# A RetNet and short-convolution decoder on one core: the norms' scales spread by transposes of whole tiles instead of products with the identity

## The chip, the core and the metric

The kernel runs on one core of a Trainium2 chip. The core has five engines with a queue each: TensorE (PE, with its weight loads as PEld), VectorE (DVE), ScalarE (ACT), GpSimd (POOL) and SyncE (SP). The engines run their own queues in order and wait for each other by semaphores. DMA transfers are issued from SP, ACT and POOL and run beside them. The metric is the device time of one execution in microseconds, the median of several runs; less is better. The granted TensorE clock is 0.999 on this core, so nothing here is throttled.

## The reference, cut to what matters

The program is one inference step of a two-layer decoder with d_model 1024 on 512 prompt tokens and 8 sequences of 4 new tokens each, together 544 token columns. Layer 0 mixes by a gated short convolution, layer 1 by retention; a SwiGLU block of width 2816 follows each; a last norm ends it.

```
def rmsnorm(x, g):
    y = xf * lax.rsqrt(jnp.mean(xf * xf, axis=-1, keepdims=True) + RMS_EPS)
    return y * g
for i in range(DEPTH):
    h = rmsnorm(x, norm_mix[i])
    m, st = short_conv_mixer(h, ...) if i % 2 == 0 else retention_mixer(h, ...)
    x = x + m
    x = x + swiglu(rmsnorm(x, norm_ffn[i]), ffn_w_gate[i], ffn_w_up[i], ffn_w_down[i])
return rmsnorm(x, final_norm), ...
```

There are five norms. Each needs, for every token, one number: the reciprocal root of the mean square over the 1024 features.

## The kernel before, in words

**Layout.** Activations lie transposed: eight tiles `x[0]` to `x[7]` of 128 features (partitions) by 544 tokens (columns). A PSUM bank holds 512 float32 columns, so the tokens are cut in two halves of `HT` = 272. A norm's scale differs by token, so by column, and must stand in every one of the 128 partitions before VectorE can multiply with it. That spread copy is the tile `R` (128 x 2 x 272).

**How a scale is made** (`rms_scale`, line 256, a generator whose steps are woven between the products of a stage). The squares are summed over the eight tiles in `sqacc`. Then five products (line 272) with `sqacc` as the stationary operand turn 128 tokens at a time from columns into a column: `ms[:, tt]` holds the means of 128 tokens, one per partition. VectorE adds epsilon (line 245), GpSimd raises to the power -1/2 (line 248), and the result is the small tile `rN` with one column per 128 tokens. To get from that column to a spread row, `spread` (line 250) takes the column `rN[:, tt]`, broadcast over 128 columns, as the stationary operand, and the identity matrix `ident` as the moving one. Six such products (lines 279 to 283) fill the two halves of 272 columns: whole tiles of 128, cut ones of 16, 112 and 32, since 272 is no multiple of 128. ScalarE copies both halves to `R` (line 284).

This happens four times: for layer 0's mixer (profiled at 34 us), layer 0's SwiGLU (206 us), layer 1's mixer (561 us, in `ahead`) and layer 1's SwiGLU (1055 us). The final norm has its own code (`scale`, line 915): each half of the tokens gets three products (lines 933 and 934), and VectorE multiplies the output straight out of PSUM (line 949); the stores follow on SP's and ACT's queues.

**The matrix products.** All large products are split: a float32 operand is written as a high part and a low part of a faster type, and three products replace one. Two weight matrices and two activation tiles at a time are multiplied by seven instead of eight block products (`Job`, line 364; products on line 386). A job's weights are prepared by `weights7` (line 320): two loads on SP's queue into tiles `w` (line 333), four sums on VectorE (lines 336 to 339), high parts on ScalarE (lines 315 and 202), and low parts in two ways. One half of a low part is a subtraction on VectorE (line 316). The other half is a negated copy on ScalarE (line 317), to which an accumulating DMA on POOL's queue adds the weight itself (line 318). A job's products come in the order 1 (first half of the first pair), then 6, 5 and 2 in an order given by the stage (2 is the second half of the first pair), 7, and at the end 3 and 4. ScalarE and VectorE add up the blocks from PSUM (lines 445 and 447). `run` (line 422) prepares the next job while the present one is multiplied.

**The order.** The program is written in one sequence, but the order on each engine is made by a scheduler that plans with its own estimates of durations, and fixed when the program is built. Pins (`issue_after`) hold a few places. A change of a few instructions can so move others far from it.

**The convolution stage**, the first, holds three plain products per feature pair, then eight jobs of the kind above. In its jobs, `take` (line 615) copies a job's last block from PSUM on ScalarE (line 618); for some jobs the convolution taps follow (lines 561 to 573), and `mixed_in` (line 576) splits the result (lines 209 to 211, with an accumulating DMA of its own).

Of the kernel before, what the change touches and what calls it, by code (L numbers as in the profile page):

```python
# [12 lines left out]
P = 128  # L13
D = 1024
KT = D // P
SEQ = 512
NB = 8
DS = 4
NS = NB * DS
# [4 lines left out]
HT = T // 2  # L24
# [28 lines left out]
def hybrid_decode_kernel(ctx: ExitStack, tc: tile.TileContext, a: dict, o: dict):  # L53
    nc = tc.nc
# [6 lines left out]
    def nm(s):  # L61
        uid[0] += 1
        return f"{s}_{uid[0]}"
# [3 lines left out]
    kinds, at = ["m"], [0]  # L67
# [5 lines left out]
    def psum():  # L73

        kind = kinds[0][at[0] % len(kinds[0])]
        at[0] += 1
        if kind == "s":
            return [bank(), bank()]
        return ps.tile([P, 2, 512], F32, tag="mm", name=nm("mm"), bufs=2)

    def bank():
        return ps.tile([P, 512], F32, tag="sm", name=nm("sm"), bufs=4)

    def half(pt, hf):
        return pt[hf] if isinstance(pt, list) else pt[:, hf, :]

    def each(fn, pt, *aps):

        if isinstance(pt, list):
            for hf in range(2):  # L90
                fn(pt[hf][:, :HT], *[ap[:, hf, :] for ap in aps])
        else:
            fn(pt[:, :, :HT], *aps)
# [6 lines left out]
    mask_s, ident, mean_w = rest[:, :NS], rest[:, NS : NS + P], rest[:, NS + P :]  # L100
# [21 lines left out]
    def g_fin(kt):  # L122
        return vec[:, 72 + kt : 73 + kt]
# [10 lines left out]
    rN = resid.tile([P, 6], F32, tag="rN", name="rN")  # L134
# [107 lines left out]
    def rsqrt(out, var, n, eps=None):  # L242

        if eps is None:
            nc.vector.tensor_scalar_add(out, var, EPS)
        else:
            nc.vector.tensor_add(out, var, eps)
        nc.gpsimd.tensor_tensor(out, out, expo[: out.shape[0], :n], op=ALU.pow)

    def spread(out, tt, lo, hi):  # L250

        return nc.tensor.matmul(
            out, rN[:, tt : tt + 1].to_broadcast([P, P]), ident[:, lo:hi], start=True, stop=True, skip_group_check=True
        )

    def rms_scale(sample=False, pt=None, rest=4):

        n = 6 if sample else 5  # L260
        pt = pt or psum()
        ms = half(pt, 0)[:, 496:502]
        cols = [slice(tt * P, (tt + 1) * P) for tt in range(4)] + [slice(T - P, T), slice(SEQ, T)]
        for tt in range(n):
            lhs = sqacc[:, cols[tt]]
            if tt == 5:
                lhs = sqlast[:, :P]
                nc.vector.tensor_copy(
                    lhs.rearrange("p (g c) -> p g c", c=NS),
                    sqacc[:, SEQ:].unsqueeze(1).to_broadcast([P, P // NS, NS]),  # L270
                )
            nc.tensor.matmul(ms[:, tt : tt + 1], lhs, mean_w[:, 0:1], start=True, stop=True)
            if tt < n - 1:
                yield
        rsqrt(rN[:, :n], ms[:, :n], n)
        for _ in range(rest):
            yield

        for tt, hf, at, lo, hi in (
            (0, 0, 0, 0, P), (1, 0, P, 0, P), (2, 0, 2 * P, 0, HT - 2 * P),  # L280
            (2, 1, 0, HT - 2 * P, P), (3, 1, 3 * P - HT, 0, P), (4, 1, SEQ - HT, P - NS, P),
        ):
            spread(half(pt, hf)[:, at : at + hi - lo], tt, lo, hi)
        each(lambda p, r: nc.scalar.activation(r, p, AF.Copy), pt, R)

    def drain(steps):
        for _ in steps:
            pass
# [165 lines left out]
    with ExitStack() as c0:  # L454
# [134 lines left out]
        c, b = temp("c"), temp("b")  # L589
        nc.gpsimd.memset(u[:, :, NSLOT : NSLOT + 2], 0.0)  # L590
        steps = rms_scale(rest=5)
        pts = [start()]
        for d, pt in zip((b, c), pts[0]):
# [68 lines left out]
        for i, n in enumerate(PAIRED[0]):  # L662
            if i < 2:
                wh, wl, pt = early[i]
                project(pt, wh, wl, 0, yh, yl, first=False, ks=(KT - 2, KT - 1))
            else:
                wh, wl = load_piece(a["cvout"][n], KT * P)
                pt = psum()
# [4 lines left out]
    def ffn(layer, next_gain, then=None):  # L673
        with ExitStack() as c1:
# [198 lines left out]
            def after(i):  # L873
                if i in behind:
                    later[behind[i]]()

            steps = rms_scale(rest=9)
            run(jobs, (5, 6, 2), after, steps)
            drain(steps)
# [8 lines left out]
    def final(ms, acts, group_weights, fp, tp):  # L888

        ah, al = acts  # L890
        ws = [group_weights(n, ms) for n in range(KT - LATE, KT)]

        sums = {}

        def products(hf):
            c = slice(hf * HT, (hf + 1) * HT)
            for n in range(KT - LATE, KT):
                wh, wl = ws[n - KT + LATE]
                pt = [None, None]
                pt[hf] = bank()  # L900
                project(pt, wh, wl, 0, ah, al, hfs=(hf,))
                nc.vector.tensor_add(x[n][:, c], x[n][:, c], half(pt, hf)[:, :HT])
                square_sum(n, tp, "gu", 4, c=c, add=nc.vector, join=not hf)
                yield

        def gained(hf):

            c = slice(hf * HT, (hf + 1) * HT)
            y = [fp.tile([P, 4, HT], F32, tag="f", name=nm("ya")), tp.tile([P, 4, HT], F32, tag="gu", name=nm("yb"))]
            for kt in range(KT):  # L910
                with tc.issue_after(last_square[0].ins) if hf and kt == KT - 2 else ExitStack():
                    nc.scalar.activation(y[kt // 4][:, kt % 4, :], x[kt][:, c], AF.Copy, scale=g_fin(kt))
            return y

        def scale(hf):
            pt = bank()
            mq = pt[:, 496:499]

            of = (sqacc, sqlast)[: hf + 1]
            for t in of:  # L920
                for i, at in enumerate((0, P, HT - P)):
                    cols = slice(hf * HT + at, hf * HT + at + P)
                    last_sum[hf] = nc.tensor.matmul(
                        mq[:, i : i + 1], t[:, cols], mean_w[:, 0:1], start=t is of[0] and (hf == 0 or i == 0),
                        stop=t is of[-1], skip_group_check=True,
                    )
                if t is not of[-1]:
                    yield
            with tc.issue_after(first_product[0].ins) if hf else ExitStack():
                nc.vector.tensor_scalar_add(rN[:, :3], mq, EPS)  # L930
            powers[hf] = nc.gpsimd.tensor_tensor(rN[:, :3], rN[:, :3], expo[:, :3], op=ALU.pow)
            yield
            for i, (lo, hi) in enumerate(((0, P), (0, P), (3 * P - HT, P))):
                last_spread[0] = spread(pt[:, i * P : i * P + hi - lo], i, lo, hi)
            sums[hf] = pt[:, :HT]

        def copied(hf):

            with tc.issue_after(last_square[0].ins):
                nc.scalar.activation(R[:, hf, :], sums[hf], AF.Copy)  # L940

        def out(hf, y, w):

            yy = y[w // 2][:, w % 2 * 2 : w % 2 * 2 + 2, :]
            if w == 0:
                for i in range(2):
                    nc.gpsimd.tensor_tensor(yy[:, i, :], yy[:, i, :], R[:, hf, :], op=ALU.mult)
            else:
                made = nc.vector.tensor_mul(yy, yy, sums[hf].unsqueeze(1).to_broadcast([P, 2, HT]))
                first_product[0] = first_product[0] or made  # L950
            q = nc.sync if w % 2 or hf == 0 else nc.scalar
            last_store[0] = q.dma_start(o["yT"][hf][:, 2 * w : 2 * w + 2], yy)

        last_sum, last_spread, powers, first_product, last_store = {}, [None], {}, [None], [None]

        def idle(n, ins):

            with tc.issue_after(ins):
                wm = bank()
                for _ in range(n):  # L960
                    last_spread[0] = nc.tensor.matmul(wm[:, :P], ones, ones, start=True, stop=True)

        drain(products(0))
        first, second = scale(0), products(1)
        next(second)
        next(first)
        y0 = gained(0)
        drain(second)
        drain(first)
        out(0, y0, 1)  # L970
        with tc.issue_after(first_product[0].ins):
            copied(0)
        rest = scale(1)
        with tc.issue_after(last_spread[0].ins):
            next(rest)
        next(rest)
        idle(5, last_sum[1].ins)
        y1 = gained(1)
        out(0, y0, 2)
        out(0, y0, 3)  # L980

        with tc.issue_after(last_store[0].ins), tc.issue_after(powers[1].ins):
            out(0, y0, 0)
        drain(rest)
        copied(1)
        for w in range(4):
            out(1, y1, w)
# [763 lines left out]
```

## Time and profile before

| | |
|---|---|
| runs | 1411.15, 1411.09, 1410.4 us |
| median | 1411.09 us |
| profiled execution, span from first to last instruction | 1409.1 us |
| PE busy | 1396.3 us (99%), 10,476 matmul records |
| DVE, ACT, POOL busy | 1132.7, 821.7 and 213.9 us |
| DMA | 233.82 MB, mean 166 GB/s |

The profiled execution is known by its span; the median of the timed runs lies 2.0 us above it, which is what stands around the first and the last instruction. The profile shows for each instruction its engine, its line, what it writes and reads, its start and its duration; in the timeline, the first column is the start and the second the duration of the (merged) row, and brackets give the idle time of the engine before it and what ended it. Matmuls overlap, so a row's duration is longer than the distance to the next row's start; that distance is what it costs.

### The profile page before, as it was taken

The page shows a single profiled execution, that of the slowest core. Times are in us where ns is not written, and L with a number is a line of the kernel's source. Part 1 is how long each engine was busy: PE and PEld are TensorE (multiplying, and loading weights), DVE is VectorE, ACT ScalarE, POOL GpSimd, SP SyncE. Part 2 cuts the span into 40 slices and gives each one's busy share as a digit, 9 for nine tenths or more (in the row PEclk, how much of TensorE's full clock was granted, in tenths as well). Part 3 has the DMA queues.
Part 4 walks back from the last instruction along what each step waited for, and adds up shares of the span by engine and source line. Part 5 has one row for each costly group of instructions (what it writes and reads, how often), then busy time and mean ns, then how long its engine had stood idle before and what let it go on. Part 6 is the DMA issues. An engine that isn't in the chain of part 4 may idle for free.

```text
span 1409.1 us, 26606 instructions
## 1 busy us (share of the span) xinstructions
PE 1396.3 (99%) x10476; PEld 1319.9 (94%) x10476; DVE 1132.7 (80%) x1929; ACT 821.7 (58%) x1281; POOL 213.9 (15%) x248
## 2 busy tenths in 40 slices
PE   9999999999999999999999999999999999999997
PEld 9999999999999999999877877887899999999997
DVE  6987879898989878767867586585798898989884
ACT  7666567677677557677532313213387767667654
POOL 0111011222221204111000000000111222121212
PEclk9999999999999999999999999999999999999999
DMA  6476347768686745677666365465676777777742
GB/s 206 121 166 166 107 110 158 173 163 185 143 196 149 171 108 158 176 199 203 197 216 232 120 212 179 139 240 179 201 152 151 168 170 172 154 184 157 163 108 87
DMA packets 99246, 233.82 MB, mean 166 GB/s; under 512 B 9744, under 2 KB 33312, under 8 KB 98736
## 3 DMA queue, kind: packets, MB, share of 16 engines
q1 hardware_dynamic: 67984, 167.60, 38.3%
q0 software_dynamic: 28688, 56.61, 23.5%
q10 hardware_dynamic: 2448, 7.91, 1.5%
q8 instruction: 82, 1.34, 0.4%
q14 instruction: 44, 0.36, 0.1%
HBM read 191.97 MB, written 28.42 MB: 156 GB/s over the span
## 4 chain that ended last, share of the span: by engine, by line
PE 93%; DVE 4%; DMA 1%; ACT 1%; issue 1%; POOL 0%; SPq 0%; DVEq 0%; POOLq 0%; ACTq 0%
PE sm L386 43%; PE mm L386 16%; PE mm L187 14%; PE sm L187 4%; PE sm L1251 2%; PE sm L1252 2%; PE sm L1253 2%; PE sm L175 2%; PE sm L177 2%; PE sm L176 1%; PE sm L1463 1%; DVE S L1486 1%; PE mm L1259 1%; PE mm L1412 0%; DVE ol L203 0%
## 5 line engine op out<-in xcount | busy, mean ns | idle before, releaser
L386 PE MATMUL sm<-oh,wh 128*128 128x272 f32 x856 | 247.8, 290 | 0.5 <-DVE b L447 0.5
L386 PE MATMUL sm<-ol,wh 128*128 128x272 f32 x856 | 246.2, 288 | 0.0
L386 PE MATMUL sm<-oh,wl 128*128 128x272 f32 x856 | 246.1, 287 | 0.0
L202 ACT ACTIVATE h<-w 128x1024 fp32r<-128x1024 f32 (+3 forms) x170 | 136.6, 804 | 105.8 <-PE mm L386 92.7
L203 DVE TENSOR_TENSOR l<-w,h 128x1024 fp32r<-128x1024 f32 (+3 forms) x170 | 153.5, 904 | 28.0 <-ACT h L202 25.0
L315 ACT ACTIVATE wh<-w 128x1024 fp32r<-128x1024 f32 (+1 forms) x134 | 133.7, 998 | 56.0 <-PE sm L386 48.3
L386 PEld LDWEIGHTS sm<-oh,wh 128*128 128x128 f32 x856 | 161.3, 188 | 2.0 <-DVE b L447 0.9
L386 PEld LDWEIGHTS sm<-oh,wl 128*128 128x128 f32 x856 | 161.1, 188 | 0.0
L386 PEld LDWEIGHTS sm<-ol,wh 128*128 128x128 f32 x856 | 160.9, 188 | 0.1
L386 PE MATMUL sm<-parts,wh 128*128 128x272 f32 x736 | 142.5, 288 | 0.0
L202 ACT ACTIVATE wh<-w 128x1024 fp32r<-128x1024 f32 (+3 forms) x76 | 67.6, 897 | 117.2 <-PE mm L187 62.0
L318 POOL DMA_DIRECT2D wl<-in_ffgu_dram x87 | 81.9, 941 | 327.9 <-ACT wl L317 135.5
L386 PE MATMUL mm<-oh,h 128*128 128x272 f32 x396 | 115.5, 292 | 0.0
L386 PEld LDWEIGHTS sm<-parts,wh 128*128 128x128 f32 x736 | 115.5, 188 | 0.0
L386 PE MATMUL mm<-oh,l 128*128 128x272 f32 x396 | 113.4, 286 | 0.0
L386 PE MATMUL mm<-ol,h 128*128 128x272 f32 x396 | 113.2, 286 | 0.0
L316 DVE TENSOR_TENSOR wl<-w,wh 128x512 fp32r<-128x512 f32 (+1 forms) x134 | 87.1, 650 | 26.5 <-ACT wh L315 26.2
L386 PE MATMUL sm<-parts,wl 128*128 128x272 f32 x368 | 106.1, 288 | 0.2 <-DMA wl<-in_rtqk_dram 0.2
L317 ACT ACTIVATE wl<-wh 128x512 fp32r<-128x512 f32 (+1 forms) x173 | 102.9, 595 | 2.0
L203 DVE TENSOR_TENSOR wl<-w,wh 128x1024 fp32r<-128x1024 f32 (+3 forms) x76 | 79.5, 1055 | 13.4 <-ACT wh L202 13.0
L187 PE MATMUL mm<-parts,wh 128*128 128x272 f32 x488 | 82.6, 291 | 0.9 <-ACT wh L202 0.9
L386 PE MATMUL sm<-oh,h 128*128 128x272 f32 x284 | 82.3, 290 | 0.3 <-ACT oh L202 0.2
(382 smaller groups left out, 3841.2 us busy)
## 6 DMA issues: line engine op xcount, KB each, us to landing
w<-in_ffgu_dram SPq DMA_DIRECT2D x66, 512.0 KB
wl<-in_ffgu_dram POOLq DMA_DIRECT2D x87, 256.0 KB, 5.2
S<-in_rets_dram SPq DMA_DIRECT2D x16, 1024.0 KB
out_rets_dram<-S SPq DMA_DIRECT2D x16, 1024.0 KB
w<-in_ffdn_dram SPq DMA_DIRECT2D x36, 384.0 KB
cb<-in_ffgu_dram SPq DMA_DIRECT2D x22, 512.0 KB
w<-in_cvin_dram SPq DMA_DIRECT2D x21, 512.0 KB
wl<-in_ffdn_dram POOLq DMA_DIRECT2D x48, 192.0 KB, 4.7
```

The lines of the kernel that those rows point to most:

```text
L175: nc.tensor.matmul(out, lh, rh, start=start, stop=False, skip_group_check=True)
L177: last_product[0] = nc.tensor.matmul(out, ll, rh, start=False, stop=stop, skip_group_check=True)
L187: last_product[0] = nc.tensor.matmul(half(pt, hf)[:, :HT], w[:, c], act[k][:, hf * HT : (hf + 1) * HT], start=(first and k == ks[0] and i ...
L202: h = nc.scalar.activation(dh, src, AF.Copy)
L203: last_low[0] = nc.vector.tensor_sub(dl, src, dh.bitcast(F32))
L315: nc.scalar.activation(wh, w, AF.Copy)
L316: last_mixed[0] = nc.vector.tensor_sub(wl[:, :n], w[:, :n], wh[:, :n].bitcast(F32))
L317: nc.scalar.activation(wl[:, n:], wh[:, n:].bitcast(F32), AF.Copy, scale=-1.0)
L318: nc.gpsimd.dma_start(wl[:, n:], src[:, 1, :] if len(src.shape) == 3 else src[:, n:], accum_op=ALU.add)
L386: last = nc.tensor.matmul(out, w[:, c], b, start=(first and j == 0 and i == 0), stop=(j == len(self.ks) - 1 and i == 2), skip_group_check= ...
L1251: nc.tensor.matmul(out, xh[kt][:, ts_], wh[:, cw], start=(kt == 0), stop=False)
L1252: nc.tensor.matmul(out, xh[kt][:, ts_], wl[:, cw], start=False, stop=False)
```

## The change

`spread` becomes a transpose of the whole broadcast tile (`tensor.transpose`, a matmul in transpose mode) where the wanted columns begin at the tile's first column, and stays a product with part of the identity where they do not. The list of cuts changes with it: whole tiles of 128 are written even where fewer columns are wanted. In the first half, tile 2 writes columns 256 to 383, of which 256 to 271 are read. In the second half, tile 2's last 112 columns stay a product, and the last tile, which holds the last 128 tokens, is written whole over columns that tile 3 has written just before with the same values. In the final norm the third spread of a half is written whole and overlaps the second.

```
-    def spread(out, tt, lo, hi):
-        return nc.tensor.matmul(
-            out, rN[:, tt : tt + 1].to_broadcast([P, P]), ident[:, lo:hi], start=True, stop=True, skip_group_check=True
-        )
+    def spread(out, tt, lo=0):
+        column = rN[:, tt : tt + 1].to_broadcast([P, P])
+        if lo == 0:
+            return nc.tensor.transpose(out, column, ident)
+        return nc.tensor.matmul(out, column, ident[:, lo:], start=True, stop=True, skip_group_check=True)
...
-        for tt, hf, at, lo, hi in (
-            (0, 0, 0, 0, P), (1, 0, P, 0, P), (2, 0, 2 * P, 0, HT - 2 * P),
-            (2, 1, 0, HT - 2 * P, P), (3, 1, 3 * P - HT, 0, P), (4, 1, SEQ - HT, P - NS, P),
+        for tt, hf, at, lo in (
+            (0, 0, 0, 0), (1, 0, P, 0), (2, 0, 2 * P, 0), (2, 1, 0, HT - 2 * P), (3, 1, 3 * P - HT, 0), (4, 1, HT - P, 0),
         ):
-            spread(half(pt, hf)[:, at : at + hi - lo], tt, lo, hi)
+            spread(half(pt, hf)[:, at : at + P - lo], tt, lo)
...
-            for i, (lo, hi) in enumerate(((0, P), (0, P), (3 * P - HT, P))):
-                last_spread[0] = spread(pt[:, i * P : i * P + hi - lo], i, lo, hi)
+            for i, at in enumerate((0, P, HT - P)):
+                last_spread[0] = spread(pt[:, at : at + P], i)
```

In all, 26 of the 30 products become transposes, and four products of 112 columns stay. The built order of the instructions changes in two ways: the edited instructions themselves, and, in the convolution stage behind the first group, the order in which PE, DVE, ACT and POOL take the work of the first jobs. SP's order and all other stages keep theirs.

## The prediction

> **What bounds the kernel now.** I read the page from its head: span, busy shares, clock, chain.
>
> ```profile
> span 1409.1 us, 26606 instructions
> PE 1396.3 (99%) x10476; PEld 1319.9 (94%) x10476; DVE 1132.7 (80%) x1929; ACT 821.7 (58%) x1281; POOL 213.9 (15%) x248
> PEclk9999999999999999999999999999999999999999
> PE 93%; DVE 4%; DMA 1%; ACT 1%; issue 1%; POOL 0%; SPq 0%; DVEq 0%; POOLq 0%; ACTq 0%
> ```
>
> TensorE is the bound nearly everywhere: 99% busy, 93% of the chain that ended last, clock granted in full. So time taken out of PE's queue shortens the kernel, and an operand that comes late lengthens it at once. Two things have to be priced: the edited instructions on PE, and the order of everything else. The built order of the changed kernel differs from that of before far from the edit, in the convolution stage.
>
> **Part 1: the four groups of six products in the norms.** The view of the spread's line counts its instructions, and the timeline shows the first group.
>
> ```profile
> L252 PE MATMUL mm<-cb,rN x36: 182/275/377, 33.9 to 1056.0; 128*128 128x128 f32 x18, 128*128 128x16 f32 x6, 128*128 128x112 f32 x6, 128*128 128x32 f32 x6
> L252 PE MATMUL sm<-cb,rN x24: 182/275/376, 561.2 to 1400.5; 128*128 128x128 f32 x14, 128*128 128x16 f32 x6, 128*128 128x112 f32 x2, 128*128 128x32 f32 x2
> ...
> 33.12 0.66 PE L187 MATMUL mm<-parts,wh 128*128 128x272 f32 x4
> 33.62 0.41 PE L187 MATMUL mm<-parts,wl 128*128 128x272 f32 x2
> 33.86 1.42 PE L252 MATMUL mm<-cb,rN 128*128 128x128 f32 x12
> 35.12 0.76 PE L187 MATMUL mm<-parts,wh 128*128 128x272 f32 x4
> 35.72 0.41 PE L187 MATMUL mm<-parts,wl 128*128 128x272 f32 x2
> ...
> 205.58 1.53 PE L252 MATMUL mm<-cb,rN 128*128 128x128 f32 x12
> 561.19 1.42 PE L252 MATMUL sm<-cb,rN 128*128 128x128 f32 x12
> 1054.83 1.42 PE L252 MATMUL mm<-cb,rN 128*128 128x128 f32 x12
> ```
>
> There are 36 + 24 = 60 matmul records for 30 products: each float32 product runs as two passes. The twelve passes hold PE from 33.86 to 35.12, 1.26 us, and the four products behind take 0.60 (35.12 to 35.72) where they usually take 0.50 (33.12 to 33.62). So a group costs 1.36 us; the other three last as long or a little longer.
>
> What a transpose costs is seen at the keys' transposes, the same instruction with the same identity:
>
> ```profile
> 705.62 1.04 PE L1306 MATMUL mm<-cb,rot 128*128 128x128 f32 x8
> 706.41 0.48 PE L1252 MATMUL sm<-wl,parts 128*128 128x512 f32 x1
> 706.73 0.40 PE L1253 MATMUL sm<-wh,parts 128*128 128x512 f32 x1
> 706.97 0.39 PE L1251 MATMUL sm<-wh,parts 128*128 128x512 f32 x1
> ```
>
> Eight records for eight transposes: one pass each. From 705.62 to 706.73 is 1.11 us, less 0.24 for the one product in between (706.73 to 706.97): 0.87, or 0.11 per transpose, entry and exit included. After the change a group is five transposes (0.55) and one 112-column product, still two passes (12 passes in 1.26 us: 0.21). That is 0.76 instead of 1.36: 0.60 less. Bounds: 0.42 (transposes at 0.14) to 0.70 (at 0.09). The whole-tile transposes write 112 columns more than the cut products (to no reader) and overwrite 96 twice, on one engine in order, so no wait is added. Three of the groups stand in stretches whose order is unchanged: -0.6 each, -1.8 us. The scales reach their readers earlier, which is worth nothing there: PE does not wait for them.
>
> **Part 2: the two groups of three at the end.**
>
> ```profile
> 1396.58 0.74 PE L252 MATMUL sm<-cb,rN 128*128 128x128 f32 x6
> 1396.78 0.44 DVE L902 TENSOR_TENSOR x<-x,sm 128x272 f32<-128x272 f32 x1
> 1397.25 0.43 ACT L234 ACTIVATE sqlast<-x 128x272 f32<-128x272 f32 x1 [0.18 <-DVE x L902]
> 1397.84 0.81 PE L923 MATMUL sm<-cb,sqlast 128*128 128x1 f32 x6
> 1399.90 0.84 PE L252 MATMUL sm<-cb,rN 128*128 128x128 f32 x6
> 1400.78 0.40 ACT L940 ACTIVATE R<-sm 128x272 f32<-128x272 f32 x1 [1.86 <-PE sm L252]
> DMA  0000000000079207999389998999996000000000
> ```
>
> The first group becomes 0.3 shorter (six passes, half of 1.26, are 0.63; three transposes, 0.33), but the last sums behind it need the squares that ACT ends at 1397.68, so only some 0.1 is gained. The second stands bare between POOL's power and the copy: 0.84 becomes 0.33 + 0.22 = 0.55, gain 0.3. Behind it the stores keep the DMA engines full (last row: 1395 to 1409.2 in 40 slices, nearly all nines from 1400.3 on), so at best the 0.4 arrives and at worst none. I take -0.25.
>
> **Part 3: the order of the convolution stage.** The first group also gives -0.6 at 34 us. But the scheduler has ordered the stage behind it anew, for some 360 products of its seven-product jobs (line 386). Job 2, the third, is where it matters. The built orders, abbreviated:
>
> ```
> ACT before: L315 wh_910 | L317 wl_911 | L202 h4_788 | L315 wh_920 | L618 h_760<-sm_747
> ACT after:  L202 h4_788 | ... L315 wh_910 | L618 h_760<-sm_747 | L317 wl_911
> PE: wl_911's second half first read by product 207 of L386 before, by product 149 after
>     job 0's last (sm_747): products 99-110 before, 104-115 after
> ```
>
> The first half of wl_911 comes from DVE and is early in both. The second half is made by ACT at L317 and then by POOL's accumulating DMA (L318). In the new order L317 stands behind L618, which waits for job 0's last product, and the reader is pulled 58 products ahead. The rows, of before:
>
> ```profile
> 57.81 0.41 PE L386 MATMUL sm<-parts,wh 128*128 128x272 f32 x2
> 72.34 0.29 PE L386 MATMUL sm<-ol,h 128*128 128x272 f32 x1
> 76.44 0.41 PE L386 MATMUL sm<-parts,wh 128*128 128x272 f32 x2
> 83.20 0.28 PE L386 MATMUL mm<-ol,h 128*128 128x272 f32 x1
> 90.08 0.29 PE L386 MATMUL sm<-oh,wl 128*128 128x272 f32 x1
> ...
> 68.72 0.63 ACT L317 ACTIVATE wl<-wh 128x512 fp32r<-128x512 f32 x1
> 71.91 1.06 ACT L315 ACTIVATE wh<-w 128x1024 fp32r<-128x1024 f32 x1 [0.88 <-PE sm L386]
> 72.87 0.38 ACT L618 ACTIVATE h<-sm 128x272 f32<-128x272 f32 x1
> 73.15 0.62 ACT L317 ACTIVATE wl<-wh 128x512 fp32r<-128x512 f32 x1
> ...
> 69.64 0.86 POOL L318 DMA_DIRECT2D wl<-in_cvin_dram  x1 [1.61 <-PE sm L386]
> ...
> DMA to landing us min/median/max: 3.7/6.5/7.7
> ...
> wl<-in_cvin_dram POOLq DMA_DIRECT2D x1, 256.0 KB, 5.4
> ```
>
> These PE rows are products 1, 115, 148-149, 200 and 255 of the stage; PE never starves here before, so place gives time. All shift by -0.6. Product 115 ends at 72.34 + 0.29 - 0.6 = 72.03. Then L618 (0.28 to the next start), L317 (0.62) and 0.29 from L317's end (69.35) to POOL's issue (69.64): issue at 73.2 instead of 69.64. Product 149 is due at 76.56 - 0.6 = 75.96. Landing takes 3.7 at the least, so PE waits at least 0.95 us; at 7.7 it waits 4.95. I take 5.4, the one issued at 54.3 (last row) with one weight load beside it, as here: landing at 78.6, **a wait of 2.65 us**. Queued behind it on PE is everything.
>
> The next job has the same pattern: its L317 now waits for product 200 (83.20 + 0.28 - 0.6 = 82.9), through L315 (0.97), L618, L317 and the issue to 85.1; the reader is product 255, due at 89.5, 4.4 later. At 3.7 it is in time, at 7.7 it costs 3.3. The engines' queue is emptier there, since a weight load has moved; I take nothing.
>
> PE being late covers later waits in turn:
>
> ```profile
> 109.82 0.52 PE L386 MATMUL mm<-parts,h 128*128 128x272 f32 x2 [0.32 <-ACT b L445]
> 114.45 0.39 PE L386 MATMUL sm<-oh,wh 128*128 128x272 f32 x1 [0.48 <-DVE b L447]
> ```
>
> If ACT and DVE are not late with PE, 0.8 us goes here; if they are, nothing. They wait for PE's sums themselves, so I take 0.4. SP's order is unchanged; on POOL one store-like accumulate (L211) moves behind a weight's, which nobody awaits within 10 us.
>
> **The sum**, against the profiled 1409.1: -0.6 + 2.65 - 0.4 in the first stage, -1.8 in three groups, -0.25 at the end: -0.4 us. The median of the runs, 1411.09, lies 2.0 above this span; I predict **1410.7 us**.
>
> **The rivals.**
> *The new wait is hidden* (20%). For it: the smallest landing, 3.7, and the two old waits. Then -0.6 - 1.8 - 0.25 = -2.65, 1408.4; with 0.8 of old waits gone, 1407.6. Against: even 3.7 leaves 0.95 in my walk.
> *The accumulating DMAs are slow* (20%, slower). With 6.5 us, the median of this stretch, in both places the waits are 3.75 and 2.1: -2.65 + 5.85 = +3.2, 1414.3. It decides from a sum of waits of 5.5 us on. Against: the queue is less crowded at 73 us than before.
> *Transposes do not pipeline* (2%). The row of L1306 gives 0.27 as one transpose's own duration; taken one after another a group costs 5 x 0.27 + 0.21 = 1.56, 0.2 more than now, and the sum of my terms becomes -0.4 + 4 x 0.8 = +2.8, 1413.9. The eight in 1.04 us speak against it, and the clock row has no dip where L1306 runs. The Trainium skill, page "TensorE: Matmul & The Clock Gate", section "Part 4: PE-mode transpose", gives about 275 ns for a transpose in one kernel and says the clock gate does not count transposes as busy, which would speak against this change; this case's trace agrees with the duration as a latency, not as a rate.
> That the change does nothing (transposes as two passes) I hold excluded: L1306 shows one record each.
>
> **How the numbers follow.** 58% the forecast (1408.6 with a landing of 3.7 and both old waits gone, to 1413.4 with 7.7 and none gone), 20% hidden, 20% slow, 2% unpipelined. What a measurement of this kernel can tell from no change is about 0.2%, 2.8 us: 1408.3 to 1413.9. The hidden case (1407.6 to 1408.4) lies for two thirds beyond its lower end, 0.13, and the forecast's lower end is nearer to it than the runs' scatter of 0.75 us, 0.03: faster 0.16. The slow case lies mostly beyond the upper end, with the unpipelined one half: 0.18, and 0.03 of the forecast's upper end in the same way: slower 0.21. The range, 1407.8 to 1414.4, reaches into both.
>
> **What would show it.** Five single records and two passes per group, PE 0.76 us in it; L618 ahead of the third job's L317; an idle time of PE near 76 us ended by DMA wl, 1 to 5 us long. Wrong it is if that wait is missing, if a second one stands near 90 us, or if waits at 110 and 114 us grow instead of shrinking.

## The result, and the profile after

The changed kernel takes 1414.74 us in the median of nine runs (1413.08 to 1415.95), the kernel before 1410.45 beside it (1409.88 to 1411.31): a ratio of 1.0028 with an interval of 1.0018 to 1.0037. It is slower by 4 us; 1410.7 was forecast, with 1414.4 as the upper end. The profiled execution of the changed kernel, at 1413.33 us one of its quicker ones, has this page; the groups' last columns are the idle time before them and what ended it.

```profile
span 1411.6 us, 26557 instructions
...
PE 1395.2 (99%) x10450; PEld 1317.2 (93%) x10450; DVE 1133.0 (80%) x1929; ACT 820.4 (58%) x1281; POOL 213.4 (15%) x248
...
PE 85%; DVE 4%; DMA 2%; ACT 1%; issue 1%; POOL 0%; DVEq 0%; SPq 0%; POOLq 0%; ACTq 0%
...
L386 PE MATMUL sm<-parts,wl 128*128 128x272 f32 x368 | 106.7, 290 | 3.2 <-DMA wl<-in_cvin_dram 3.0
```

PE's busy time has become 1.1 us less (1396.3 before), the span 2.5 us more: what was saved is there, and more has been lost in waiting. The chain holds DMA for 2% instead of 1%. (PE's share of it, 85% against 93%, is 91% in the second trace of the same kernel, so nothing is read from it.) The list of PE's waits (total, times, longest) names them:

```profile
PE sm L386 <- DMA wl<-in_cvin_dram: 3.0, 1, 3.0
PE sm L485 <- DVE expo L108: 1.1, 1, 1.1
PE sm L386 <- DVE c L447: 0.8, 1, 0.8
PE mm L187 <- ACT wh L202: 0.5, 1, 0.5
```

The first and the third are new; the waits of before for `b` (L445 and L447) are gone. The timeline shows the first one as the prediction walked it: L618 ahead of L317, the DMA issued at 73.82, PE at the reader from 75.7 on, and its work resumed at 78.91, 5.1 us after the issue. What holds L618 is L315 ahead of it on ACT, which waited for PE until 71.67.

```profile
71.67 1.06 ACT L315 ACTIVATE wh<-w 128x1024 fp32r<-128x1024 f32 x1 [4.17 <-PE sm L386]
72.63 0.38 ACT L618 ACTIVATE h<-sm 128x272 f32<-128x272 f32 x1
72.91 0.62 ACT L317 ACTIVATE wl<-wh 128x512 fp32r<-128x512 f32 x1
73.82 0.86 POOL L318 DMA_DIRECT2D wl<-in_cvin_dram  x1 [6.26 <-ACT wl L317]
75.47 0.41 PE L386 MATMUL sm<-parts,wh 128*128 128x272 f32 x2
78.91 0.39 PE L386 MATMUL sm<-parts,wl 128*128 128x272 f32 x1 [3.02 <-DMA wl<-in_cvin_dram]
```

The third, near 96 us, was not forecast. VectorE's addition to `c`, for which PE waits, stands in the new order behind two sums of the next weights, and the first of those waits for its load:

```profile
94.50 0.69 DVE L337 TENSOR_TENSOR w<-w,w 128x512 f32<-128x512 f32 x1 [1.02 <-DMA w<-in_cvin_dram]
95.11 0.69 DVE L338 TENSOR_TENSOR w<-w,w 128x512 f32<-128x512 f32 x1
95.71 0.43 DVE L447 TENSOR_TENSOR c<-c,sm 128x272 f32<-128x272 f32 x1
...
96.20 0.40 PE L386 MATMUL sm<-oh,wh 128*128 128x272 f32 x1 [0.80 <-DVE c L447]
```

The edited groups cost what was worked out. The first group of the changed kernel:

```profile
33.54 0.49 PE L254 MATMUL mm<-cb,rN 128*128 128x128 f32 x3
33.87 0.37 PE L255 MATMUL mm<-cb,rN 128*128 128x112 f32 x2
34.08 0.38 PE L254 MATMUL mm<-cb,rN 128*128 128x128 f32 x2
34.21 0.74 PE L187 MATMUL mm<-parts,wh 128*128 128x272 f32 x4
34.79 0.41 PE L187 MATMUL mm<-parts,wl 128*128 128x272 f32 x2
```

Five records for five transposes; 33.54 to 34.21 is 0.67, and the four products behind take 0.08 more than their 0.50: 0.75 instead of 1.36.

The groups stand in a fixed place of the program and so mark its stages. The table gives the start of each on PE (the first row of line 254 or, before, 252) in all traces that are compared below.

| trace | group 1 | group 2 | group 3 | group 4 | end, 1st | end, 2nd | span |
|---|---|---|---|---|---|---|---|
| before | 33.86 | 205.58 | 561.19 | 1054.83 | 1396.58 | 1399.90 | 1409.1 |
| before, again | 33.65 | 204.70 | 560.35 | 1054.32 | 1396.15 | 1399.47 | 1408.7 |
| changed | 33.54 | 208.47 | 563.52 | 1057.89 | 1399.11 | 1402.35 | 1411.6 |
| changed, again | 33.84 | 207.93 | 562.89 | 1057.65 | 1398.80 | 1402.03 | 1411.2 |
| changed, third | 33.62 | 210.09 | 565.07 | 1058.98 | 1400.15 | 1403.39 | 1412.6 |
| one transpose | 34.17 | 210.43 | 566.03 | 1060.28 | 1402.01 | 1405.33 | 1414.5 |
| order kept | 34.06 | 204.74 | 559.69 | 1052.34 | 1393.48 | 1396.72 | 1405.9 |
| order kept, again | 33.80 | 204.69 | 559.67 | 1053.30 | 1394.47 | 1397.71 | 1406.9 |
| three groups and end | 33.06 | 204.37 | 559.32 | 1053.22 | 1394.37 | 1397.60 | 1406.8 |
| reader held | 32.67 | 205.73 | 560.72 | 1054.76 | 1395.95 | 1399.19 | 1408.4 |

From group 1 to group 2, which holds the convolution stage and group 1 itself, it is 171.7 and 171.1 us in the two traces of before, and 174.9, 174.1 and 176.5 in the three of the changed kernel: 2.4 to 5.4 us more. From group 3 to group 4 the changed kernel takes as long as before or up to 1.1 us longer, which is taken up below; the other stages are shorter or equal.

### The profile page after: what moved, and what is told of

It is laid out like the page before. It is cut to its first block, busy times and chain, and to the rows that moved or that the text cites. A ratio compares the mean times of both kernels' runs of the same rounds, so it can differ in the third digit from the quotient of the medians.

```text
span 1411.6 us, 26557 instructions
## 1 busy us (share of the span) xinstructions
PE 1395.2 (99%) x10450; PEld 1317.2 (93%) x10450; DVE 1133.0 (80%) x1929; ACT 820.4 (58%) x1281; POOL 213.4 (15%) x248
## 4 chain that ended last, share of the span: by engine, by line
PE 85%; DVE 4%; DMA 2%; ACT 1%; issue 1%; POOL 0%; DVEq 0%; SPq 0%; POOLq 0%; ACTq 0%
PE sm L386 42%; PE mm L386 16%; PE mm L187 11%; PE sm L187 2%; PE sm L1251 2%; PE sm L1252 2%; PE sm L1253 2%; PE sm L175 2%; PE sm L177 1%; PE sm L176 1%; PE sm L1463 1%; DVE S L1486 1%; DMA rot<-km 1%; PE mm L1259 0%; PE mm L1412 0%
## 5 line engine op out<-in xcount | busy, mean ns | idle before, releaser
L386 PE MATMUL sm<-oh,wh 128*128 128x272 f32 x856 | 248.0, 290 | 0.8 <-DVE c L447 0.8
L386 PE MATMUL sm<-ol,wh 128*128 128x272 f32 x856 | 246.1, 288 | 0.0
L386 PE MATMUL sm<-oh,wl 128*128 128x272 f32 x856 | 246.0, 287 | 0.0
L202 ACT ACTIVATE h<-w 128x1024 fp32r<-128x1024 f32 (+3 forms) x170 | 136.5, 804 | 103.9 <-PE mm L386 91.7
L203 DVE TENSOR_TENSOR l<-w,h 128x1024 fp32r<-128x1024 f32 (+3 forms) x170 | 153.5, 904 | 25.9 <-ACT h L202 22.9
L315 ACT ACTIVATE wh<-w 128x1024 fp32r<-128x1024 f32 (+1 forms) x134 | 133.7, 998 | 62.4 <-PE sm L386 55.0
L386 PEld LDWEIGHTS sm<-oh,wh 128*128 128x128 f32 x856 | 161.3, 188 | 2.6 <-DVE c L447 1.0
L386 PEld LDWEIGHTS sm<-oh,wl 128*128 128x128 f32 x856 | 161.1, 188 | 0.0
L386 PEld LDWEIGHTS sm<-ol,wh 128*128 128x128 f32 x856 | 160.9, 188 | 0.1
L386 PE MATMUL sm<-parts,wh 128*128 128x272 f32 x736 | 142.8, 288 | 0.0
L202 ACT ACTIVATE wh<-w 128x1024 fp32r<-128x1024 f32 (+3 forms) x76 | 67.5, 896 | 115.8 <-PE mm L187 62.4
L386 PEld LDWEIGHTS sm<-parts,wh 128*128 128x128 f32 x736 | 115.6, 188 | 0.0
L386 PE MATMUL mm<-oh,h 128*128 128x272 f32 x396 | 115.6, 292 | 0.0
L386 PE MATMUL mm<-oh,l 128*128 128x272 f32 x396 | 113.5, 287 | 0.0
L386 PE MATMUL mm<-ol,h 128*128 128x272 f32 x396 | 113.3, 286 | 0.0
L386 PE MATMUL sm<-parts,wl 128*128 128x272 f32 x368 | 106.7, 290 | 3.2 <-DMA wl<-in_cvin_dram 3.0
L317 ACT ACTIVATE wl<-wh 128x512 fp32r<-128x512 f32 (+1 forms) x173 | 102.8, 594 | 1.9
L203 DVE TENSOR_TENSOR wl<-w,wh 128x1024 fp32r<-128x1024 f32 (+3 forms) x76 | 79.6, 1055 | 12.5 <-ACT wh L202 12.2
L386 PE MATMUL sm<-oh,h 128*128 128x272 f32 x284 | 82.2, 290 | 0.5 <-ACT g L445 0.3
```

What stands on the lines that cost most here:

```text
L202: h = nc.scalar.activation(dh, src, AF.Copy)
L203: last_low[0] = nc.vector.tensor_sub(dl, src, dh.bitcast(F32))
L315: nc.scalar.activation(wh, w, AF.Copy)
L317: nc.scalar.activation(wl[:, n:], wh[:, n:].bitcast(F32), AF.Copy, scale=-1.0)
L386: last = nc.tensor.matmul(out, w[:, c], b, start=(first and j == 0 and i == 0), stop=(j == len(self.ks) - 1 and i == 2), skip_group_check= ...
```

## The experiments

**Transposes or order?** The scheduler orders the convolution stage anew for some choices of the six spreads of the first group, and not for others. That allows two kernels that separate the two halves of the change. The first makes a single spread a transpose and gets the changed kernel's orders on DVE, ACT and POOL:

```
-steps = rms_scale(rest=5)
+steps = rms_scale(rest=5, sel=(
+    (0, 0, 0, 0, P, 0), (1, 0, P, 0, P, 1), (2, 0, 2 * P, 0, HT - 2 * P, 1),
+    (2, 1, 0, HT - 2 * P, P, 1), (3, 1, 3 * P - HT, 0, P, 1), (4, 1, SEQ - HT, P - NS, P, 1)))
```

In the last field 1 is a product with the identity and 0 a transpose; all other groups keep their products.

> A single one of the 30 spread products becomes a transpose: the first of the first group. All others stay products with the identity. The built order of DVE, ACT and POOL is that of the changed kernel, since the scheduler orders the convolution stage anew already for this one edit. Theory (the order of the convolution stage costs the time, the transposes save it): about 0.1 us saved at 34 us, then the waits of the changed kernel, near 76 us for a DMA (2 to 5 us) and near 95 us for DVE (0.8): 3.5 to 5 us slower than before, 1414 to 1415.5, so as slow as or slower than the changed kernel although 25 of its 26 transposes are missing. Rival (transposes cost time themselves, by about 4.3/26 = 0.17 us each): 1410.6. Rival (the attention part of the changed kernel, 1.3 us later between 590 and 1040 us, is a consequence of its transposes there): no such 1.3 here, where before it is only scatter.

Measured: 1416.31 (1414.16 to 1417.1) against 1410.82, a ratio of 1.0037 (1.0025 to 1.005). One transpose costs as much as the 26, by the median even more; the two intervals overlap. The number, 0.8 us above the forecast's upper end, is that of an execution with a stretch at half clock, of which more below. Its waits:

```profile
PE sm L386 <- DMA wl<-in_cvin_dram: 3.0, 1, 3.0
PE mm L187 <- ACT wh L202: 1.2, 1, 1.2
PE sm L485 <- DVE expo L108: 1.1, 1, 1.1
PE sm L386 <- DVE c L447: 0.5, 1, 0.5
```

The second has the order of before and all transposes of the changed kernel but one, the fifth spread of the first group. That makes 25 of 26; the expectations below say 24, a miscount.

```
-(3, 1, 3 * P - HT, 0, P, 0)
+(3, 1, 3 * P - HT, 0, P, 1)
```

> 24 of the changed kernel's 26 transposes are there; in the first group two of the six spreads stay products (112 columns of the third tile, as in the changed kernel, and the fourth tile's 128), and only with this the scheduler gives ACT, POOL and SP the order of before. Theory (the order costs, the transposes save): 0.4 saved in the first group, 0.6 in each of three others, 0 to 0.3 at the end: 2.2 to 2.5 us faster than before, 1408.1, with no wait for a DMA near 76 us. Rival (transposes cost time themselves, 0.17 us each): 4 us slower than before, 1414.5. Rival (attention part): about 1.3 us slower than the theory says, 1409.4, and the later events again between 590 and 1040 us.

> 24 transposes with the order of before, once more, for the size of its gain. By the traced steps 2.2 us: 0.4 in the first group, 0.6 in each of three others; the first measurement gave 1.4 (0.1 to 2.7 by its interval). Theory: again 1 to 2.2 us faster than before. Rival (the transposes cost something in the part from 590 to 1040 us, where six of the eight traces with them are 0.8 to 1.7 us late): again only 1.4 or less, and that part late by 0.5 us or more against the traces of before.

Measured: 1409.38 against 1410.82, 0.9990 (0.9981 to 0.9999), and the second time 1409.89 against 1410.8, 0.9992 (0.9983 to 1.0001). PE does not wait for the convolution's weights here; the two old waits for `b` are back:

```profile
PE sm L386 <- DVE b L447: 0.5, 1, 0.5
PE mm L187 <- ACT wh L202: 0.3, 1, 0.3
PE mm L386 <- ACT b L445: 0.3, 1, 0.3
```

So the order costs and the transposes save; the rivals by which the transposes cost time themselves fall. The gain is 0.9 to 1.4 us where the steps gave 2.2, and the second interval just reaches 1. The first number, 1409.38, is also that of the rival on the attention part, and the gain of the second is what its own rival named. The late events that both rivals ask for are not in these two traces, which take 492.7 and 493.6 us from group 3 to group 4, against 493.6 and 494.0 before; that stage is taken up below. The third kernel leaves all of the first group as it was:

```
-steps = rms_scale(rest=5)
+steps = rms_scale(rest=5, cut=True)   # six products here; transposes in the other groups and at the end
```

> The first group keeps its six products; the three other groups and the two at the end have the transposes. ACT, POOL and SP have the order of before, PE's and DVE's differ only in the edited instructions. Theory: 1.8 us faster in three groups, 0 to 0.3 at the end: 1408.4, and 0.4 slower than with the transposes in the first group and the order kept. Rival (transposes cost time themselves): 1414.

Measured: 1409.54, 0.9989 (0.9980 to 0.9997): the sign as expected, the gain 1.3 of 1.8 to 2.1. It cannot be told from the kernel with the order kept.

**What scatters?** The changed kernel's runs lie up to 4.4 us apart, those of before beside them up to 2.0.

> The changed kernel once more, for a second trace. Theory: 1414.7 again; PE's wait near 76 us for the accumulating DMA varies with the landing (2 to 5 us), and that is what makes this kernel's runs scatter more than those of before; the 1.3 us between 590 and 1040 us is scatter of one trace and is not seen again in the same places. Rival (it belongs to the change): the same 1.3 us at the same places, 600, 705, 875 and 920 us.

> The changed kernel, a third trace. Theory (half clock behind the wait in 13 of 20 executions): two chances in three that the trace shows one stretch of 3.4 us at half clock right behind the 3.0 us wait near 79 us, products at 0.23 instead of 0.125 us apart, and then a span near 1413; otherwise a span near 1411.3. Rival (the landing scatters): the DMA lands more than 0.5 us later or earlier than the 5.0 to 5.1 us of the two traces so far, and the span moves by that.

Measured: 1414.34 (1411.82 to 1416.23), 1.0025 (1.0016 to 1.0034), and 1414.38 in the single third run. In all three traces the wait is 3.0 to 3.1 us and the DMA lands 5.0 to 5.1 us after its issue: the landing, in these traces, does not scatter. The third trace shows what does. Its stretches by time, with their length, PE's busy time and records, the granted clock, the DMA share and GB/s:

```profile
70.00:76.00 6.00, 5.90 (x48) 1.00 0.69 156
76.00:79.00 3.00, 0.04 (x1) 0.96 0.58 111
79.00:82.00 3.00, 3.00 (x13) 0.50 0.88 152
82.00:86.00 4.00, 4.00 (x33) 0.98 0.22 87
```

And PE's timeline, with some like rows left out:

```profile
78.96 0.59 PE L386 MATMUL sm<-parts,wl 128*128 128x272 f32 x1 [3.06 <-DMA wl<-in_cvin_dram]
79.35 0.43 PE L386 MATMUL mm<-oh,l 128*128 128x272 f32 x1
79.58 0.43 PE L386 MATMUL mm<-oh,h 128*128 128x272 f32 x1
...
82.25 0.28 PE L386 MATMUL sm<-ol,wh 128*128 128x272 f32 x1
82.37 0.29 PE L386 MATMUL sm<-oh,wl 128*128 128x272 f32 x1
```

Behind the wait the clock is granted by half: products come every 0.23 us and not every 0.125, until 82.2. The clock record of the trace has this stretch from 78.75 us on, 3.413 us long; half of it, 1.7, is the most that it can cost. The same stretch stands behind the wait in the trace of the kernel with one transpose, not in the first two of the changed kernel. Of the 21 executions of the changed kernel, 14 have a mean granted clock of 0.997 or less, and their spans average 1413.0; the 7 at 0.998 average 1411.3. The difference is 1.6 us. (Of the 84 executions of the kernel before that have a clock on record, none is under 0.998.) The first trace is one of the seven; the median of the runs is one with the stretch, and this is why it lies 1.4 us above the traced execution.

The length of the wait does not decide whether the stretch comes, since it is 3.0 us with and without it. The traces show what does differ. In the clock records of all 13 traces, every stretch but the last is a whole multiple of 3.413 us long, so that the clock changes only at the boundaries of a grid of that step, and the grid lies differently against the program in each execution. This is PE's idle time by that grid around the wait in each trace that has one:

| trace | stretch of the grid (us) | PE idle in it | clock in the next stretch |
|---|---|---|---|
| changed | 73.79 to 77.20 | 1.3 | 1.0 |
| | 77.20 to 80.62 | 1.7 | 1.0 |
| changed, again | 74.42 to 77.83 | 1.6 | 1.0 |
| | 77.83 to 81.25 | 1.3 | 1.0 |
| changed, third | 75.34 to 78.75 | 2.9 | 0.5 |
| one transpose | 76.16 to 79.57 | 2.6 | 0.5 |
| wait lengthened (below) | 78.49 to 81.90 | 2.1 | 0.5 |
| wait shortened (below) | 78.31 to 81.73 | 1.0 | 1.0 |

Where a boundary cuts the wait into 1.3 and 1.6 or 1.7 us, the clock stays whole; where 2.1 us or more fall into one stretch, the next one runs at half clock. No other place of the 13 traces speaks against this. As an estimate from these rows, a wait that falls anywhere in the grid with equal chance gets the half clock in 66 to 88% of executions when it is 3.0 us long, and in 45 to 67% when it is 2.3 us; 14 of 21 and, below, 7 of 11 were measured. The Trainium skill, page "TensorE: Matmul & The Clock Gate", section "Part 1: The HAM clock gate", describes a free-running window of 3413 ns and a half clock after an idle window of about 3.4 us. The traces agree on the length and on a window that does not start with the program, and differ in that 2.1 us of idle time within one window were already enough.

Two kernels were to change the length of the idle time alone. The first holds the waiting products back behind ten ready ones:

```
 self.b = bank()[:, :HT]
-self.product(self.b, 2, True)
+with tc.issue_after(Job.made[5].ins) if self.hold else ExitStack():   # hold: third job only
+    self.product(self.b, 2, True)
```

> The changed kernel with the same three products held behind the job's own block 5, 10 ready products or 1.25 us of work. The DMA's issue and landing are not touched, so PE should go on at the same moment near 79 us as in the changed kernel; only its idle time is 1.7 us instead of 3.0, since it does ready work in the meantime. Theory (the scatter of the changed kernel, 1411.8 to 1416.2, comes from the clock: an idle time of 3 us can cost TensorE one stretch of 3.4 us at half clock, as the trace of the kernel with one transpose shows at 80 to 83 us, up to 1.7 us): no such stretch here, the fastest runs like the changed kernel's fastest, the slow ones gone: median 1413.0, highest under 1414.3. Rival (the scatter comes from when the DMA lands): median 1414.3 and the same 4 us of scatter. Rival (the length of the idle time is itself the cost): everything 1.25 us earlier, fastest run near 1410.6.

Measured: 1412.09 (1410.75 to 1414.62), 1.0009 (1.0000 to 1.0018). One execution of 11 is at 0.997, none below: the half clock is all but gone, as the theory says. But the median is 0.9 lower than forecast, and the ten executions at 0.998 and more average a span of 1410.0, 1.3 less than those of the changed kernel; the third reading, a shorter idle time as a gain in itself, has that number. In the profiled execution PE resumes when the DMA lands, as in the changed kernel, and that span is no shorter (1411.6). Why the other executions are quicker is open.

The second puts one more instruction on POOL ahead of the DMA:

```
 nc.scalar.activation(wl[:, n:], wh[:, n:].bitcast(F32), AF.Copy, scale=-1.0)
+nc.gpsimd.tensor_tensor(expo[:, 8:11], ones[:, :3], wl[:, n : n + 3].bitcast(F32), op=ALU.pow)   # third job, first pair
 nc.gpsimd.dma_start(wl[:, n:], src[:, n:], accum_op=ALU.add)
```

> The changed kernel with one more instruction in all: a power of 128x3 numbers on POOL (0.85 to 1.0 us in the norms' rows), which reads what L317 has written of the third job's wl and stands ahead of the accumulating DMA. The order on every engine is that of the changed kernel otherwise. It lengthens PE's idle time near 76 us from 3.0 to about 4.0 us. Theory (half clock behind long idle times): of the 20 executions of the changed kernel 13 have a mean clock of 0.997 or less and a mean span of 1413.0, the other 7 have 0.998 and 1411.3; the 1.7 between is one stretch of 3.4 us at half clock. With 4 us nearly every execution gets it: median span 1411.3 + 1.0 + 1.7 = 1414.0, time 1415.7, hardly any execution at 0.998, the fastest no longer under 1413.5. Rival (the scatter comes from the landing): all executions 1.0 later, clock distribution as before: median 1415.3, fastest 1412.8.

Measured: 1413.31 (1412.28 to 1415.4), 1.0018 (1.0009 to 1.0027): a miss. The order was not quite that of the changed kernel: the one waiting product also moved behind ten ready ones. PE's idle time fell into 0.4 us before those and 2.3 behind them, with the resumption at 80.6. The trace has a half-clock stretch again (from about 82 to 85 us), and 7 of 11 executions are at 0.997 or less. So it tells nothing of longer waits, but something of shorter ones: an idle time of 2.3 us, of which 2.1 fall into one stretch of the grid, can be enough, while that of 1.0 us in the kernel above was so in at most 1 of 11.

**Which half of the order?** The late L317, or the reader pulled forward? Here the reader is held behind the previous job's block 3; ACT's and POOL's orders stay as changed.

```
+with tc.issue_after(Job.made[3].ins) if self.hold else ExitStack():   # hold: third job only
+    self.product(self.b, 2, True)
```

> The changed kernel with one pin: the products of the third job's block 2, whose third reads the second half of wl_911, may not be issued before the previous job's block 3 is. ACT's and POOL's orders through the third job stay those of the changed kernel (L317 still behind L618, the DMA still issued near 74 us); on PE 60 ready products move ahead of the reader, 7 us of work. Theory (the reader pulled forward makes the wait): PE's wait for the DMA near 76 us is gone, its 3.0 us with it, and with it whatever slows single executions by a half clock behind it; the wait for DVE near 95 us (0.2 to 0.8) stays or gives way to the old ones: 1409.5, between 1408.5 and 1410.5. Rival (the late L317 itself is what costs: all later work of ACT, POOL and the next jobs' weights is late with it): the wait moves to a later reader and the time stays at 1413 to 1414.5.

Measured: 1411.59 (1410.06 to 1412.58), 1.0003 (0.9995 to 1.0012). The 3.0 us are gone, and so are executions under 0.998. But the stage is not as short as before: 173.1 us from group 1 to group 2, with the transposes' gain in it. Smaller waits have come up:

```profile
PE mm L386 <- DVE l L203: 0.6, 1, 0.6
PE sm L386 <- DVE b L447: 0.5, 1, 0.5
PE sm L386 <- DVE c L447: 0.5, 1, 0.5
```

The first of these stands at 75.4 us:

```profile
72.50 1.22 DVE L624 TENSOR_TENSOR u<-c,h 128x1024 f32<-128x1024 f32 x1
72.56 1.05 ACT L202 ACTIVATE h<-w 128x1024 fp32r<-128x1024 f32 x1
...
74.12 1.21 DVE L203 TENSOR_TENSOR l<-w,h 128x1024 fp32r<-128x1024 f32 x1
...
75.39 0.39 PE L386 MATMUL mm<-oh,l 128*128 128x272 f32 x1 [0.62 <-DVE l L203]
```

PE waits for the low part that VectorE makes at L203. ACT's L202, which follows L317 and L618 and from which the low part is made, has ended at 73.61; L203 starts 0.5 us later, because it stands on VectorE's queue behind L624 and two more operations. In the changed kernel it was covered by the longer wait. Neither theory was wholly right. Without the half clock the pulled reader makes 1.0 to 1.9 us of the stage (174.1 and 174.9 less 173.1). The other 1.3 to 2.0 us against before stay, although the transposes' 0.6 is gained in this stage too; the waits above are part of them.

A kernel without a pin, whose first group is issued two steps later, keeps L317 behind L618 and does not pull the reader:

```
-steps = rms_scale(rest=5)
+steps = rms_scale(rest=7)
```

> The changed kernel, all 26 transposes in, with the first group issued two steps of the weaving later (rest=7 instead of 5). The scheduler gives a third order of the convolution stage: L317 of the third job stands behind L618 as in the changed kernel, but the reader of its second half is not pulled forward. Theory: no wait of PE for that DMA, the transposes' 2.4 us are kept: 1408.5 to 1410. Rival (L317 behind L618 costs in itself): 1413 or more.

Measured: 1411.41 (1409.48 to 1413.71), 1.0004 (0.9995 to 1.0012), 1.4 over the forecast's upper end. The DMA's wait is missing, but this order has its own, ahead of the third job. VectorE's addition to `h` stands behind sums of weights whose load is late:

```profile
69.22 0.69 DVE L337 TENSOR_TENSOR w<-w,w 128x512 f32<-128x512 f32 x1 [2.21 <-DMA w<-in_cvin_dram]
...
71.39 0.43 DVE L447 TENSOR_TENSOR h<-h,mm 128x272 f32<-128x272 f32 x1
...
71.52 0.39 PE L386 MATMUL sm<-oh,wh 128*128 128x272 f32 x1 [1.31 <-DVE h L447]
```

Where each order loses its time can be counted by place, as the prediction did. The table gives how much later than in the first trace of before the n-th product of L386 starts, each counted from group 1 of its own trace (us; a minus sign is earlier). With the first group issued later, products change sides with it, so that only the changes within the last column count.

| n | changed | again | third | order kept | reader held | later first group |
|---|---|---|---|---|---|---|
| 90 | -0.6 | -0.6 | -0.6 | -0.6 | -0.6 | -1.1 |
| 148 | -0.5 | -0.5 | -0.6 | -0.5 | 0.4 | 0.5 |
| 149 | 2.7 | 2.6 | 2.6 | -0.5 | 0.4 | 0.5 |
| 200 | 2.5 | 2.5 | 3.9 | -0.6 | 0.4 | 0.4 |
| 270 | 2.7 | 2.6 | 4.1 | -0.6 | 0.8 | 0.4 |
| 290 | 3.8 | 3.0 | 5.2 | -0.6 | 1.5 | 0.4 |
| 400 | 4.3 | 3.5 | 5.6 | -0.6 | 1.8 | 0.4 |
| 450 | 3.2 | 2.4 | 4.8 | -0.6 | 1.4 | 0.2 |

With the order of before, the transposes' 0.6 stays as it is through the stage. The kernel with the later first group loses 1.6 us between products 90 and 148, at its wait for `h`, and nothing behind them, although its L317 stands behind L618 too (at 74.45 behind 74.17). So a late L317 alone costs nothing there. The reader-held kernel loses 0.9 us up to product 148, at its wait for `l`, and 1.4 more up to 400, more than half of it at its wait for `c` (products 270 to 290); no run takes this apart further.

**The stage between groups 3 and 4.** The first trace of the changed kernel came 1.3 us late there.

> The kernel before once more, for a second trace. The part from 590 to 1040 us came 1.3 us late in the changed kernel's trace against the one trace of before. Theory (scatter of that one trace of before): against it, this trace too is 0.3 to 1.3 us late in that part, with the same order of instructions. Rival (it belongs to the change): no difference above 0.3 us there.

Measured: 1410.47. The second trace is 0.3 us later in that part, at the border between theory and rival, so that it decides nothing. From group 3 to group 4 it is 493.6 and 494.0 us in the two traces of before and 494.3 in the kernel with one transpose, which has none there. Group 3 should make that 0.6 less. It is 494.4, 494.8, 493.9, 492.7, 493.6, 493.9 and 494.0 in the seven traces of the table that have it: 493.9 in the mean, no less than without. The group itself is shorter in each; its gain does not reach group 4 on average. Between single traces the stage scatters by 2 us, so that this is an indication and no more. A part of the scatter has a name: the second trace of the changed kernel waits 1.0 us for `gate` (L1418) near 928 us, where the first waits 0.2.

## Why the prediction was wrong, by its steps

**Part 1 was right in size, and partly in what it is worth.** A group takes 0.75 (0.76 forecast). From group 2 to group 3 it is 355.6 in both traces of before and 355.0 to 355.1 in all three of the changed kernel; from group 4 to the end's first group 341.8 and 341.2. Each is the 0.6. Group 3's 0.6 is not seen at group 4. The sentence "which is worth nothing there: PE does not wait for them" holds for the scales; that PE's saved time always shortens the kernel does not hold for that stage as measured.

**Part 2 was right in its first term and failed in its second.** From the end's first group to its second it is 3.32 before and 3.24 after: 0.08, where 0.1 was forecast. The 0.3 behind the second group arrived at ScalarE's copy (2.15 us later than before instead of 2.45) and not at the end: from the second group to the last instruction it is 9.2 us in both. By the times of the rows the last store waits for POOL, not for the spread. In the changed kernel:

```profile
1401.44 0.85 POOL L931 TENSOR_TENSOR rN<-rN,expo 128x3 f32<-128x3 f32 x1 [4.00 <-DVE rN L930]
...
1402.27 2.91 POOL L947 TENSOR_TENSOR ya<-ya,R 128x272 f32<-128x272 f32 x4
1402.35 0.54 PE L254 MATMUL sm<-cb,rN 128*128 128x128 f32 x3
1402.93 0.40 ACT L940 ACTIVATE R<-sm 128x272 f32<-128x272 f32 x1 [1.60 <-PE sm L254]
...
1405.20 0.34 ACTq L952 DMA_DIRECT2D out_yT_dram<-ya  x1
...
1405.64 0.42 ACTq L952 DMA_DIRECT2D out_yT_dram<-yb  x1
```

POOL's four products follow its power without a gap and take 2.91 us, as they did before from 1399.82 on. They end at 1405.18; the store of their result is issued from ACT's queue at 1405.20, and ACT's last store stands behind it, at 1403.20 before and at 1405.64 now, 2.44 later. VectorE's half of the output, which the spread does release, was stored at 1403.25 before and at 1405.40 now, 2.15 later. The prediction looked for the bound of the tail in the DMA engines and passed over POOL.

**Part 3 had the first wait right and stopped there.** Its place (76 us), its cause and nearly its size (2.65 forecast; 3.0 of idle time, and 3.2 counted by place as the forecast was; issue at 73.8 instead of 73.2, reader due at 75.7 instead of 76.0, landing 5.1 instead of 5.4) came out. The issue was later than walked because L618 stood behind L315 and not behind job 0's last product alone. The rival of slow accumulating DMAs, whose number 1414.3 the result hits, is not what happened, and the agreement is chance: landings were 5.1, not 6.5, and the next job's DMA, issued at 87.76 in the first trace and landed after 3.9 us, was there 0.8 us ahead of its reader (product 255, at 92.45).

The table by place shows what was missed. VectorE's addition to `c` behind the weights' sums costs 1.1, 0.3 and 1.0 us in the three traces (products 270 to 290); the walk had followed the moved ACT and POOL instructions and not those of DVE. Another 0.5 us up to product 400 goes in steps for which the profile lists no wait. The two old waits went whole, 0.9 to 1.1 us in place and not 0.4. And the half clock behind the wait stands in no term: 1.4 us in the third trace against the other two (products 149 to 200), and by the spans 1.6 us in two executions of three, so 1.1 in the mean. The clock row of before had no dip, and the forecast took a wait to cost its own length. None of the three signs that were to show the prediction wrong appeared.

The failed step is thus the sum of the first stage, -0.6 + 2.65 - 0.4 = +1.65 forecast, where the three traces show +2.4 to +5.4 against the two of before. In the first trace it is, by place, -0.5 + 3.2 + 1.1 + 0.5 - 1.1 = +3.2, and in the third the half clock comes on top. With it fall 0.6 of Part 1, some 0.2 of Part 2, and "The median of the runs, 1411.09, lies 2.0 above this span" as a rule: an execution of the kernel before takes 1.7 to 1.8 us more than its own span, and the median of the changed kernel lies 3.2 above its first traced span, which has no half clock. Not explained are some 0.4 to 0.9 us in the version with the order kept, which gains 0.9 to 1.4 where its visible steps (0.45, 0.6, 0.6 and 0.1) give 1.8; the one with three groups gains 1.3, as its steps do.

## What to carry to other kernels

Where a scheduler orders the program, price an edit by the order that it makes: here one transpose of 0.1 us moved 360 products, and which of six spreads are edited decided between 1 us gained and 4 or more lost. A wait of PE of 2 to 3 us can have a second price behind it, a stretch at half clock, and whether it does can differ from one execution to the next; read the clock in more than one trace. A wait removed uncovers the smaller ones that it hid. In a tail, ask for the last instruction what releases it, before counting what becomes shorter ahead of it.

## What the runs showed of the hardware

TensorE's clock on this single core, else granted in full while it works, changed only at the boundaries of a grid of 3.413 us that lies differently in each execution. It fell to half for one stretch of the grid where PE had been idle for 2.1, 2.6 and 2.9 us of the stretch before, and stayed whole behind stretches with up to 1.7 us of idle time. So one and the same wait of 3.0 us did and did not cost it. By the mean clock it came in 14 of 21 executions of the same program with that wait, in 7 of 11 where the wait was 2.3 us, in 1 of 11 where it was 1.0 us, and in none of 11 each where the longest wait of the stage was 0.6 or 1.3 us.

Transposes of 128x128 float32 in a row followed each other every 0.11 us (three from 33.54 to 33.87), where the product with the identity ran as two passes of 0.105 us each; one transpose alone has a duration of 0.27 us.
